# Reordering the last MLP pass of an encoder kernel: up and down visits, norm sums issued later, last squares summed by fp32 matmuls

## Chip, cores, metric

The kernel runs on the 8 cores of one Trainium2 chip. Every core computes two of the 16 sequences. The metric is device time in microseconds (us) of the slowest core. A program on all cores has a fast and a slow state: in the slow one the cores of a die are granted a lower clock (0.918 against 0.998 in the slow run of the result below). Fast runs are compared with fast runs here.

Most of the evidence is a shorter measure, read from each core's trace: **the last stretch**, from the first Relu of the last pass to the end of the core's span. Everything that the change touches lies in it, but for one memset of 0.17 us just before, and it repeats within 0.2 us over the eight cores of one execution of the kernel before or after, whereas the whole span varies by 4 to 6 us over cores, because the cores reach the last pass at different times.

## The reference, cut to what matters

```python
def rms_norm(x, g):
    y = xf * lax.rsqrt(jnp.mean(xf * xf, axis=-1, keepdims=True) + EPS)
    return (y * g).astype(x.dtype)

x = x + sq_relu_mlp(h, w_up, w_down)     # a = relu(h @ w_up);  (a * a) @ w_down
return rms_norm(x, norm_final)           # D_MODEL 1024, D_FF 4096, SEQ 2048
```

The kernel does the MLP in four passes of 1024 hidden channels. A pass visits four groups of 512 positions, each with an `up` and a `down` (8 tiles of 8 matmuls). In the last pass each `down` tile ends with the final residual add, and the final norm follows. The norm needs the sum of the squares over the 1024 channels, which lie in 8 chunks of 128 partitions, so the sum over partitions is a matmul with ones. The last group goes down in two halves of 256 positions.

## The kernel before

```python
def norm_sq(k, src, n=512, ns=0, eng='pool', lag=False, bufs=None):   # chunk k of 8
    # (cut: views of acc_, hi, lo, sq_)
    act(sq_[k % 2][:, 0:n] if k else acc_, src, AF.Square)            # ScalarE
    # (cut: the unused lag)
    add(k)                                                            # GpSimd: acc_ += sq_
    if k == 7:
        act(hi, acc_, AF.Copy)                                        # bf16 part
        tt('dve', lo, acc_, hi, ALU.subtract)                         # the rest, bf16

def norm_rstd(n=512, ns=0, r=None):                                   # "the sums"
    mm(o, ones, hi[:, 0:n], True, False)
    mm(o, ones, lo[:, 0:n], False, True)
    act(r, o, AF.Ln, scale=1.0 / D, bias=eps)
    act(r, r, AF.Exp, scale=-0.5)

def popp(fc, first=3, steps=2):      # after tile fc: `steps` pieces of pending work, from tile `first` on
    ...

def down(p_, tg, t0=0, n=512):
    first = 1 + last_seq if p_ == 3 else 3
    for fc in range(8):
        # (cut: 8 matmuls into o)
        tt('dve', x_, o, x_, ALU.add)                                 # VectorE: the add
        if p_ == 3:
            norm_sq(fc, x_, n, 0 if n == 512 else t0 // 256)
        popp(fc, first)

def fin_out(tg, t0=0, n=512, b_=b_):                                  # pending work of a finished group
    norm_rstd(n, ns, r)
    yield
    for c in range(8):
        stt(x_, x_, gains[:, 4, c:c + 1], r, ALU.mult, ALU.mult)      # VectorE: a scaling
        # (cut: every second chunk a store)
        yield

# last pass of the last sequence
for tg in range(NTG):
    up(3, tg)
    if tg:
        down(3, tg - 1)
        pend.append(fin_out(tg - 1))
for t0 in (0, 256):
    down(3, 3, t0, 256)
    pend.append(fin_out(3, t0, 256))
flush()
```

The softmax here doesn't subtract the row's maximum and nothing guards it: scores larger than these inputs give would overflow.

## Time and profile before

| | before |
|---|---|
| recorded runs | 2020.15, 2088.87, 1993.32 us, median 2020.15 |
| profiled run | 1995.15 us, fast; spans of the cores 1987.8 to 1994.1 us |
| last stretch | 132.8 us (132.7 to 132.9 over the cores) |
| of it: first Relu to last add | 121.2 us |
| of it: last add to the end | 11.6 us |

The page (slowest core, 5), busy time of TensorE, and shares of the chain of work that ended last:

```profile
PE 1957.0 (98%) x10234; PEld 968.8 (49%) x10234; DVE 963.5 (48%) x1585; ACT 773.3 (39%) x1291; POOL 417.5 (21%) x384
...
PE 93%; DVE 2%; SPq 1%; DMA 1%; issue 1%; ACT 1%; POOL 0%; DVEq 0%; ACTq 0%; POOLq 0%
```

TensorE (PE) bounds the kernel as a whole. The same chain from 1950 us on, by engine:

```profile
by line: DVE arena L149 29.9%; PE ps L149 19.9%; issue 15.9%; ACT arena L149 14.3%; POOL arena L149 7.7%; DVEq L143 1.5%; ACTq L143 0.5%; POOLq L143 0.3%
```

The timeline of TensorE (columns: start, length, engine, line, operation, tiles and shape, count, then in brackets the idle time before and what ended it):

```profile
1889.80 69.69 PE L149 MATMUL ps<-arena 128*128 128x512 bf16 x334
1960.89 0.38 PE L149 MATMUL ps<-arena 128*128 128x512 bf16 x1 [1.40 <-ACT arena L149]
1961.71 7.36 PE L149 MATMUL ps<-arena 128*128 128x512 bf16 x65 [0.45 <-DVE arena L149]
1974.26 0.37 PE L149 MATMUL ps<-arena 128*128 128x256 bf16 x1 [5.19 <-ACT arena L149]
1974.82 6.20 PE L149 MATMUL ps<-arena 128*128 128x256 bf16 x41 [0.18 <-DVE arena L149]
1985.09 0.86 PE L149 MATMUL ps<-arena 128*128 128x256 bf16 x2 [4.07 <-ACT arena L149]
```

Two waits stand out: at 1959.5 for hi and lo of group 2, at 1969.1 for those of the first half of group 3. After the second, 41 matmuls take 6.20 us where 65 had taken 7.36: their records start 0.213 us apart instead of 0.109 until 1978.1. The granted clock in three stretches (columns: stretch, length, busy time and count of TensorE, weight loads, VectorE, ScalarE, GpSimd, then granted clock, DMA share, GB/s):

```profile
1790.00:1887.00 97.00, 97.00 (x452) 43.94 (x450) 30.47 (x56) 18.51 (x31) 1.59 (x3) 1.00 0.18 33
1962.00:1969.00 7.00, 7.00 (x65) 6.09 (x63) 5.02 (x10) 3.12 (x7) 3.54 (x4) 1.00 0.19 77
...
1975.00:1982.00 7.00, 6.02 (x41) 4.61 (x39) 5.45 (x15) 3.11 (x8) 3.56 (x5) 0.78 0.22 75
```

The end on VectorE: adds (arena<-ps,arena, they read PSUM), scalings (SCALAR_TENSOR_TENSOR), and one lo (bf16<-f32).

```profile
1977.22 0.64 DVE L149 SCALAR_TENSOR_TENSOR arena<-arena 128x256 f32<-128x256 f32 x1 [1.55 <-ACT arena L149]
1977.79 0.41 DVE L149 TENSOR_TENSOR arena<-ps,arena 128x256 f32<-128x256 f32 x1
1978.12 0.87 DVE L149 SCALAR_TENSOR_TENSOR arena<-arena 128x256 f32<-128x256 f32 x2
1978.91 0.41 DVE L149 TENSOR_TENSOR arena<-ps,arena 128x256 f32<-128x256 f32 x1
...
1982.42 0.41 DVE L149 TENSOR_TENSOR arena<-ps,arena 128x256 f32<-128x256 f32 x1
1985.01 0.43 DVE L149 TENSOR_TENSOR arena<-arena 128x256 bf16<-128x256 f32 x1 [2.17 <-ACT arena L149]
1987.20 3.26 DVE L149 SCALAR_TENSOR_TENSOR arena<-arena 128x256 f32<-128x256 f32 x8 [1.77 <-ACT arena L149]
```

From 1977.22 to the last add at 1982.42 VectorE never idles: two scalings and an add per tile. The start of the last stretch, on ScalarE:

```profile
1861.25 0.60 ACT L149 ACTIVATE arena<-ps 128x512 bf16<-128x512 f32 x1 [28.76 <-PE ps L149]
```

So on this core the last stretch is 1994.1 - 1861.25 = 132.8 us, and the last add comes 1982.42 - 1861.25 = 121.2 us after its start.

### The profile page before, as it was taken

To read this page: it belongs to the slowest core of one execution; us is meant where nothing else is said; L and a number is where in the kernel's file an instruction comes from. 1 tells how busy PE (TensorE), PEld (TensorE's weight loads), DVE (VectorE), ACT (ScalarE), POOL (GpSimd) and SP (SyncE) were. 2 spreads that over 40 slices of the span, in tenths; PEclk is the share of its full clock that TensorE was granted. 3 is DMA by queue.
4 is the path that set the end of the run, shared out by engine and by line. 5 is a ranking of instruction groups with operands and counts; after the bars stand their busy time and mean duration, and the time that the engine had idled before them with its cause. 6 is when DMAs were issued, how large, how long until landed. Compare 5 with 4: busy or idle time off the path is not lost.

```text
span 1994.1 us, 30646 instructions; the slowest of 8 cores (1987.8 to 1994.1 us)
## 1 busy us (share of the span) xinstructions
PE 1957.0 (98%) x10234; PEld 968.8 (49%) x10234; DVE 963.5 (48%) x1585; ACT 773.3 (39%) x1291; POOL 417.5 (21%) x384
## 2 busy tenths in 40 slices
PE   8999999999999999999999999999999999999996
PEld 4456544554444444444445664446444444444443
DVE  5955643455553333336764456335556332323355
ACT  6355742455431332213325557235554112021243
POOL 3001042531310321101420002344133000000034
PEclk9999999999999999999999999999999999999998
DMA  9472352663012525043372440635600040222112
GB/s 239 85 138 64 54 139 73 106 110 60 1 64 43 118 69 110 22 79 116 102 198 60 86 81 23 189 59 96 121 1 1 1 79 6 46 40 43 22 75 95
DMA packets 51738, 155.41 MB, mean 78 GB/s; under 512 B 4993, under 2 KB 15362, under 8 KB 42114
## 3 DMA queue, kind: packets, MB, share of 16 engines
q0 software_dynamic: 14416, 75.50, 22.2%
q1 hardware_dynamic: 37026, 77.94, 12.6%
q8 instruction: 86, 1.41, 0.3%
q14 instruction: 66, 0.54, 0.1%
q10 hardware_dynamic: 144, 0.02, 0.0%
HBM read 205.87 MB, written 16.78 MB: 112 GB/s over the span
## 4 chain that ended last, share of the span: by engine, by line
PE 93%; DVE 2%; SPq 1%; DMA 1%; issue 1%; ACT 1%; POOL 0%; DVEq 0%; ACTq 0%; POOLq 0%
PE ps L149 93%; DVE arena L149 2%; SPq L149 1%; DMA arena<-x 1%; ACT arena L149 1%; DMA arena<-arena 0%; POOL arena L149 0%; SPq L147 0%; DVEq L143 0%; ACTq L143 0%; POOLq L143 0%; SPq L143 0%
## 5 line engine op out<-in xcount | busy, mean ns | idle before, releaser
L149 PE MATMUL ps<-arena 128*128 128x512 bf16 (+4 forms) x10234 | 1957.0, 354 | 28.9 <-ACT arena L149 12.0
L149 PEld LDWEIGHTS ps<-arena 128*128 128x128 bf16 (+1 forms) x10234 | 968.8, 100 | 1016.8 <-issue 70.1
L149 ACT ACTIVATE arena<-ps 128x512 bf16<-128x512 f32 (+3 forms) x776 | 472.4, 631 | 869.7 <-PE ps L149 747.7
L149 DVE TENSOR_TENSOR arena<-arena 128x512 bf16<-128x512 bf16 (+8 forms) x597 | 305.9, 532 | 479.3 <-ACT arena L149 466.5
L149 POOL TENSOR_TENSOR arena<-arena 128x512 f32<-128x512 f32 (+2 forms) x289 | 358.2, 1242 | 697.4 <-ACT arena L149 484.5
L149 DVE TENSOR_TENSOR arena<-ps,arena 128x512 f32<-128x512 f32 (+4 forms) x394 | 280.2, 722 | 280.2 <-PE ps L149 270.6
L149 ACT ACTIVATE arena<-arena 128x512 f32<-128x512 f32 (+6 forms) x460 | 282.4, 625 | 299.8 <-DVE arena L149 198.3
L149 DVE SCALAR_TENSOR_TENSOR arena<-arena 128x512 bf16<-128x512 f32 (+3 forms) x312 | 215.6, 730 | 37.8 <-ACT arena L149 37.3
L149 POOL DMA_DIRECT2D arena<-wb x62 | 33.8, 547 | 641.2 <-PE ps L149 602.7
L149 DVE SCALAR_TENSOR_TENSOR arena<-arena,ps 128x512 f32<-128x512 f32 x128 | 80.6, 683 | 126.9 <-PE ps L149 121.3
L149 DVE SCALAR_TENSOR_TENSOR arena<-ps,arena 128x512 f32<-128x512 f32 x64 | 43.5, 687 | 32.9 <-PE ps L149 32.9
L149 ACT ACTIVATE arena<-ps,arena 128x512 f32<-128x512 f32 (+3 forms) x50 | 29.2, 585 | 40.1 <-PE ps L149 35.6
L149 DVE COPY arena<-ps 128x1024 f32<-128x1024 f32 (+3 forms) x20 | 20.2, 1010 | 37.6 <-PE ps L149 37.6
L149 POOL DMA_DIRECT2D arena<-wa x23 | 15.6, 683 | 106.9 <-PE ps L149 87.2
L149 POOL MEMSET arena<- 128x2048 bf16 x6 | 10.8, 1808 | 120.8 <-PE ps L149 120.8
L149 DVE CAST arena<-ps 128x512 bf16<-128x512 f32 (+1 forms) x30 | 19.6, 667 | 12.1 <-PE ps L149 12.0
L149 DVE STREAM_SHUFFLE arena<-arena 128x2048 bf16<-128x2048 bf16 x6 | 13.7, 2287 | 0.0
L149 ACT ACT_TABLE_LOAD x5 | 6.4, 1283 | 4.1 <-DVE arena L149 4.1
L149 DVE TENSOR_SCALAR arena<-arena 128x512 bf16<-128x512 f32 x12 | 6.1, 516 | 3.3 <-DMA arena<-x 3.2
L149 DVE LOAD_MASK_SELECT arena<-arena x6 | 0.1, 14 | 13.2 <-DMA arena<-arena 13.1
L149 DVE MEMSET arena<- 128x1 bf16 (+3 forms) x7 | 0.9, 135 | 3.3 <-DMA arena<-gains 2.1
L149 DVE CAST arena<-arena 128x1 bf16<-128x1 f32 (+1 forms) x9 | 1.4, 160 | 0.4
(4 smaller groups left out, 0.4 us busy)
## 6 DMA issues: line engine op xcount, KB each, us to landing
arena<-wb POOLq DMA_DIRECT2D x62, 1024.0 KB, 9.9
arena<-x SPq DMA_DIRECT2D x8, 2048.0 KB, 24.5
arena<-x SPq DMA_DIRECT2D x32, 512.0 KB, 3.8
out<-arena SPq DMA_DIRECT2D x28, 512.0 KB, 2.8
arena<-wa POOLq DMA_DIRECT2D x17, 512.0 KB, 9.5
arena<-x SPq DMA_DIRECT2D x32, 256.0 KB, 14.7
arena<-rope SPq DMA_DIRECT2D x6, 1024.0 KB, 6.4
arena<-arena SPq DMA_DIRECT2D x96, 64.0 KB, 2.3
```

Of the source, the lines that this page charges most:

```text
L149: ins = getattr(eo, o['name'])(*o['args'], **o['kw'])
```

## The change

Four parts, all in the last pass of the last sequence. The visits become up0, up1, down0, up2, down1, down2, up3, down3, so that group 2's scalings run beside up3, and 14 of down3's matmuls are issued ahead of the last squared tile. The sums are issued later in TensorE's order (after tile 3 or 4 instead of 2). One chunk of the first half and three of the second go into the sums by fp32 matmuls with fp32 ones instead of GpSimd adds. One scaling per tile instead of two in the halves.

```diff
+        ones32_ = view(OFF['Y'] + 12 * KB, 128, F32)
+        sq_last = [[view(OFF['Y'] + (3 * i + k) * KB, 256, F32) for k in range(3)] for i in range(2)]
+            if k == (6 if direct == 3 else 8):
+                split()                                   # hi, lo
+            if k >= 8 - direct:
+                act(sq_last[ns][k - 8 + direct][:, 0:n], src, AF.Square)
+            elif k: ...                                   # Square, GpSimd add
+            if k == 7 and direct < 3:
+                split()
             mm(o, ones, hi[:, 0:n], True, False)
-            mm(o, ones, lo[:, 0:n], False, True)
+            mm(o, ones, lo[:, 0:n], False, direct == 0)
+            for k in range(direct):
+                mm(o, ones32_, sq_last[ns][k][:, 0:n], False, k == direct - 1)
...
-                first = 1 + last_seq if p_ == 3 else ...
+                first = (4 if tg == 3 else 2) if p_ == 3 and last_seq else ...      # in up
...
+                late = direct == 1
+                if late:
+                    for fc in range(2):
+                        tile_mm(fc, range(7))
-                    popp(fc, first)
+                    popp(fc, first, 1 if direct else 2)
...
-                yield
+                for _ in range(2 if direct else 1):
+                    yield
...
+                up(3, 0)
+                for tg in range(NTG - 1):
+                    if tg < NTG - 2:
+                        up(3, tg + 1)
+                    down(3, tg)
+                    pend.append(fin_out(tg))
+                up(3, 3)
+                for k, direct in enumerate((1, 3)):
+                    down(3, 3, 256 * k, 256, k, 3, direct)
+                    pend.append(fin_out(3, 256 * k, 256, k, direct))
```

(Cut: views, `tile_mm`, which issues the matmuls of one tile, the memset of the fp32 ones, and the old loop. Other passes and the first sequence keep their order.)

More of the change, by code (lines that the diff above doesn't have):

```diff
@@ L327, in wdma, with norm_sq, split, norm_rstd @@
             return dma('pool', dst, src, 'w%d' % (wn[0] % 10), after)
-        def norm_sq(k, src, n=512, ns=0, eng='pool', lag=False, bufs=None):
+        ones32_ = view(OFF['Y'] + 12 * KB, 128, F32)
+        sq_last = [[view(OFF['Y'] + (3 * i + k) * KB, 256, F32) for k in range(3)] for i in range(2)]
+        def norm_sq(k, src, n=512, ns=0, bufs=None, direct=0):
             acc_, (hi, lo) = nset[ns]
             acc_, hi, lo = acc_[:, 0:n], hi[:, 0:n], lo[:, 0:n]
-            sq_ = sq if bufs is None else bufs
-            def add(i):
-                if i > 0:
-                    tt(eng, acc_, acc_, sq_[i % 2][:, 0:n], ALU.add)
-            act(sq_[k % 2][:, 0:n] if k else acc_, src, AF.Square)
-            if lag and k:
-                add(k - 1)
-            if not lag or k == 7:
-                add(k)
-            if k == 7:
+            sq_ = (sq if bufs is None else bufs)[k % 2][:, 0:n]
+            def split():
                 act(hi, acc_, AF.Copy)
                 tt('dve', lo, acc_, hi, ALU.subtract)
-        def norm_rstd(n=512, ns=0, r=None):
+            if k == (6 if direct == 3 else 8):
+                split()
+            if k >= 8 - direct:
+                act(sq_last[ns][k - 8 + direct][:, 0:n], src, AF.Square)
+            elif k:
+                act(sq_, src, AF.Square)
+                tt('pool', acc_, acc_, sq_, ALU.add)
+            else:
+                act(acc_, src, AF.Square)
+            if k == 7 and direct < 3:
+                split()
+        def norm_rstd(n=512, ns=0, r=None, direct=0):
             r = (rstd if r is None else r)[:, 0:n]
@@ L1207, in up @@
             def up(p_, tg, hook=None):
-                first = 1 + last_seq if p_ == 3 else 6 if p_ + tg == 0 else 3
+                first = (4 if tg == 3 else 2) if p_ == 3 and last_seq else 1 if p_ == 3 else 6 if p_ + tg == 0 else 3
                 for fc in range(8):
@@ L1220, in up, with down, tile_mm, fin_out @@
                     popp(fc, first)
-            def down(p_, tg, t0=0, n=512):
-                first = 1 + last_seq if p_ == 3 else 3
+            def down(p_, tg, t0=0, n=512, ns=0, first=None, direct=0):
+                if first is None:
+                    first = 1 + last_seq if p_ == 3 else 3
                 tn = slice(t0, t0 + n)
-                for fc in range(8):
-                    w = bslot(17 + 4 * p_ + fc // 4).rearrange("p (k j) -> p k j", k=8)
-                    b = P.bank()
-                    o = psf(b)[:, 0:n]
-                    for dc in range(8):
-                        mm(o, w[:, dc, (fc % 4) * 128:(fc % 4 + 1) * 128], a2T[tg % 2][:, dc, tn], dc == 0, dc == 7)
+                bank = {}
+                late = direct == 1
+                def tile_mm(fc, dcs):
+                    if fc not in bank:
+                        bank[fc] = P.bank()
+                    w = bslot(17 + 4 * p_ + fc // 4).rearrange("p (k j) -> p k j", k=8)
+                    for dc in dcs:
+                        mm(psf(bank[fc])[:, 0:n], w[:, dc, (fc % 4) * 128:(fc % 4 + 1) * 128], a2T[tg % 2][:, dc, tn], dc == 0, dc == 7)
+                if late:
+                    for fc in range(2):
+                        tile_mm(fc, range(7))
+                for fc in range(8):
+                    tile_mm(fc, (7,) if late and fc < 2 else range(8))
                     x_ = xT[:, tg, fc, tn]
-                    tt('dve', x_, o, x_, ALU.add)
+                    tt('dve', x_, psf(bank[fc])[:, 0:n], x_, ALU.add)
                     if p_ == 3:
-                        norm_sq(fc, x_, n, 0 if n == 512 else t0 // 256)
-                    popp(fc, first)
+                        norm_sq(fc, x_, n, ns, direct=direct)
+                    popp(fc, first, 1 if direct else 2)
             rstd2 = view(Y0 + 8192, 512, F32)
-            def fin_out(tg, t0=0, n=512, b_=b_):
+            def fin_out(tg, t0=0, n=512, ns=0, direct=0, b_=b_):
                 tn = slice(t0, t0 + n)
-                ns = 0 if n == 512 else t0 // 256
                 r = (rstd, rstd2)[ns][:, 0:n]
-                norm_rstd(n, ns, r)
-                yield
+                norm_rstd(n, ns, r, direct)
+                for _ in range(2 if direct else 1):
+                    yield
                 for c in range(8):
@@ L1323, in build_program @@
                 aload(1)
+            if last_seq:
+                OP('dve', 'memset', ones32_, 1.0, writes=[ones32_])
+                up(3, 0)
[8 more added lines that the diff above has]
+                    pend.append(fin_out(3, 256 * k, 256, k, direct))
+                flush()
+                continue
             for tg in range(NTG):
                 up(3, tg)
-                if not last_seq:
-                    pend.append(fin_next(tg))
-                    if tg == 3:
-                        aload(2)
-                        aload(3)
+                pend.append(fin_next(tg))
+                if tg == 3:
+                    aload(2)
+                    aload(3)
                 if tg:
@@ L1333, in build_program @@
                     pend.append(fin_out(tg - 1))
-            if last_seq:
-                for t0 in (0, 256):
-                    down(3, 3, t0, 256)
-                    pend.append(fin_out(3, t0, 256))
-                flush()
-            else:
-                down(3, 3)
-                flush()
-                pend.append(fin_out(3))
-                load_rope(0)
-                for i in range(4, 8):
-                    aload(i)
+            down(3, 3)
+            flush()
+            pend.append(fin_out(3))
+            load_rope(0)
+            for i in range(4, 8):
+                aload(i)
         sems = []
```

## The prediction

> **What bounds it.** TensorE: busy 98% of the 1994.1 us span (page), 93% of the chain that ended last. Only the last 40 us are loose. In the last pass of the last sequence TensorE is dense until 1959.5. The waits view from 1880 on gives it 7.2 us idle in two places: 1.4+0.45 us at 1959.5 (sums of position group 2, issued three 256-wide tiles after that group's last add) and 5.2 us at 1969.1 (sums of group 3's first half, same distance). Behind the second gap matmuls start 0.213 us apart instead of 0.109 until 1978.1: the half clock after idleness of the Trainium skill, "TensorE: Matmul & The Clock Gate", Part 1; the trace agrees (PEclk 0.78 there). That costs another 1.7 us. VectorE, given two scalings per tile, is then 1.4 us behind: last matmul ends 1981.0, last add starts 1982.4. Then (timeline): square, two GpSimd adds (0.73 us each), hi, lo, two matmuls, Ln, Exp; scalings start 1987.2, 4.8 us after that add, take 3.3 us; the store lands 3.6 us later.
>
> **What changes.**
> 1. Group 3's up comes after group 2's down, so group 2's sums are issued five up tiles (8.6 us) after their chain starts, which needs about 4: that gap goes. Group 3's down now follows its up at once; the last squared tile is ready about 1.3 us after the last up matmul, and 14 matmuls held before it cover 1.5: 0 to 0.3 us lost.
> 2. The first half's sums come after four tiles (3.5 us) and the chain is shorter: chunk 7's square by one fp32 matmul instead of a GpSimd add, hi/lo ready about 2 us after the last matmul. The 5.2 us and the half clock go.
> 3. One scaling per tile, from tile 5: no VectorE backlog.
> 4. Second half: chunks 5 to 7 by fp32 matmuls; hi/lo done during the visit. After the last add: square 0.42, one fp32 matmul, Ln 0.47, Exp 0.42.
>
> **Costs added.** Four fp32 matmuls of 256 columns. The kernel's start has 512-column ones: two records 0.50 us apart, 1.09 together, against 0.216 bf16 spacing; the skill's "FP8 and Floating Point Precision" gives four passes, which agrees. Estimate 0.5 us each. One lies on the dense path, two run beside add and square, one in the tail. Five left-over scalings of the first half (2 us on VectorE) fall in the tail beside square, matmul, Ln, Exp: 0 to 0.3 us.
>
> **Sum (slowest core).** Down of group 3 starts 1957.1, 128 matmuls at 0.109, plus 0.75 for the first half's sums: last matmul ends 1972.1 (8.9 earlier); last add 1972.2 (10.2 earlier); scalings about 2.9 after it instead of 4.8: 1975.1; then 3.3 + 3.6 unchanged: 1982. About 12 us, 0.6%, all on the critical path.
>
> **Predicted**: 1982.5 us in the fast state (before, fast: 1993 to 1995), 1979 to 1987 there. The recorded 2020 median of before contains slow runs; if after's does too, it reads about 12 us under its like. So the range is 1979 to 2010. Faster by over 2%: 0.03; within 2%: 0.96; slower: 0.01.
>
> **What would show it.** TensorE waits after 1950 down from 7.2 us to under 1, apart from the tail; clock 0.99 in the 15 us before the last add, at 1972 to 1973; GpSimd absent from the final chain, one fp32 matmul in its place; last add to first scaling about 3 us.
>
> **What would make it wrong.** The 14 held matmuls don't cover; fp32 matmuls slower than estimated; VectorE behind in group 2's down (0.69 + two scalings 1.41 exceeds 1.73 us per tile); left-over scalings or their stores delaying the final ones; GpSimd behind in the first half, so that its sums wait.

## The result

| | before | after |
|---|---|---|
| median of all runs | 2007.09 us (4) | 1984.09 us (4) |
| those at the fast level | 1993.32, 1994.03 | 1983.35, 1984.77, 1983.4, and 1985.58, which the median leaves out |
| ratio of fast runs, 95% interval | | 0.9953 (0.9929 to 0.9977) |
| the same, later with more rounds | | 0.9956 (0.9943 to 0.9970) |
| last stretch, every core | 132.8 us | 123.5 us |
| first Relu to last add | 121.2 us | 113.6 us |
| last add to the end | 11.6 us | 9.9 us |

A ratio is the mean time of one kernel's fast runs over that of the other's, the 1985.58 us counted too, so not quite the ratio of the medians. The gain is 9.3 us in the last stretch, on each of the eight cores, and 9.3 of 1993.7 us is the 0.47% of the ratio. One of the new kernel's runs was slow (2139.22 us: die 0 at a clock of 0.918, die 1 at 0.998); it is left out.

After (slowest core, 4), the start of the last stretch on ScalarE:

```profile
1858.76 0.60 ACT L149 ACTIVATE arena<-ps 128x512 bf16<-128x512 f32 x1 [28.76 <-PE ps L149]
```

The timeline of TensorE after:

```profile
1939.76 9.68 PE L149 MATMUL ps<-arena 128*128 128x512 bf16 x43
1949.89 7.08 PE L149 MATMUL ps<-arena 128*128 128x512 bf16 x39 [0.45 <-DVE arena L149]
1957.27 13.37 PE L149 MATMUL ps<-arena 128*128 128x256 bf16 x118 [0.29 <-DVE arena L149]
1971.72 0.27 PE L149 MATMUL ps<-arena 128*128 128x256 bf16 x1 [1.08 <-ACT arena L149]
1972.21 1.91 PE L149 MATMUL ps<-arena 128*128 128x256 bf16 x7 [0.22 <-DVE arena L149]
```

The waits of 1.4 and 5.2 us are gone, and no matmul before the tail runs at the half clock. What is left: a small wait for group 2's lo at 1949.4, one at 1957.0 where the held matmuls have run out, and 1.08 us for hi at 1970.6, after the last visit. The first of them is a little longer than its bracket: matmul records overlap, and single records show a start 0.83 us after the one before where 0.216 is usual, so 0.6 us is lost; in the second 0.46 us (0.567 instead of 0.109).

GpSimd in the last two visits (six and four adds):

```profile
1959.77 5.35 POOL L149 TENSOR_TENSOR arena<-arena 128x256 f32<-128x256 f32 x6 [11.68 <-ACT arena L149]
1967.61 3.35 POOL L149 TENSOR_TENSOR arena<-arena 128x256 f32<-128x256 f32 x4 [2.49 <-ACT arena L149]
```

Within each half it adds without a pause, about 0.9 us from start to start, as long as TensorE takes for a tile (8 matmuls of 0.109 us); between the halves it waits 2.49 us. VectorE, in group 2's down, between the halves and at the end:

```profile
1938.17 0.68 DVE L149 TENSOR_TENSOR arena<-ps,arena 128x512 f32<-128x512 f32 x1
1938.77 2.87 DVE L149 SCALAR_TENSOR_TENSOR arena<-arena 128x512 f32<-128x512 f32 x2
1941.56 0.68 DVE L149 TENSOR_TENSOR arena<-ps,arena 128x512 f32<-128x512 f32 x1
...
1965.86 0.43 DVE L149 TENSOR_TENSOR arena<-arena 128x256 bf16<-128x256 f32 x1 [2.45 <-ACT arena L149]
1966.21 1.41 DVE L149 TENSOR_TENSOR arena<-ps,arena 128x256 f32<-128x256 f32 x4
...
1970.29 0.42 DVE L149 TENSOR_TENSOR arena<-ps,arena 128x256 f32<-128x256 f32 x1
1971.63 0.43 DVE L149 TENSOR_TENSOR arena<-arena 128x256 bf16<-128x256 f32 x1 [0.93 <-ACT arena L149]
1971.98 0.48 DVE L149 SCALAR_TENSOR_TENSOR arena<-arena 128x256 f32<-128x256 f32 x1
1972.37 0.42 DVE L149 TENSOR_TENSOR arena<-ps,arena 128x256 f32<-128x256 f32 x1
1972.71 2.45 DVE L149 SCALAR_TENSOR_TENSOR arena<-arena 128x256 f32<-128x256 f32 x6
1975.37 3.25 DVE L149 SCALAR_TENSOR_TENSOR arena<-arena 128x256 f32<-128x256 f32 x8 [0.20 <-ACT arena L149]
```

The line at 1965.86 is the first half's lo. VectorE idles 2.45 us before it, and the second half's first adds stand behind it, although that half's first tile had its last matmul at 1963.49: this is why GpSimd, which needs their squares, pauses between the halves. The line at 1971.63 is the second half's lo. It stands before the last add (1972.37) in VectorE's order, and it waits for hi, which waits for GpSimd. The last matmul of the visit had started at 1970.36, so its add could have begun at about 1970.7. And two scalings at 1938.77 take 2.87 us where two usually take 1.41. The chain from 1950 on:

```profile
by line: DVE arena L149 17.6%; POOL arena L149 17.0%; ACT arena L149 11.9%; issue 11.2%; PE ps L149 4.9%; DVEq L143 1.0%; POOLq L143 0.4%; ACTq L143 0.3%
```

GpSimd's (POOL) share rose from 7.7% to 17.0%: it was predicted to leave the chain, and now stands level with VectorE's 17.6% at the front of it.

### The profile page after: what moved, and what is told of

The parts are those of the page before. It is cut to its first block, busy times and chain, and to the rows that moved or that the text cites. A ratio compares the mean times of both kernels' runs of the same rounds, so it can differ in the third digit from the quotient of the medians.

```text
span 1982.3 us, 30478 instructions; the slowest of 8 cores (1978.4 to 1982.3 us)
## 1 busy us (share of the span) xinstructions
PE 1944.4 (98%) x10062; PEld 968.3 (49%) x10242; DVE 963.9 (49%) x1586; ACT 772.5 (39%) x1291; POOL 414.1 (21%) x380
## 3 DMA queue, kind: packets, MB, share of 16 engines
q8 instruction: 86, 1.41, 0.3%
## 4 chain that ended last, share of the span: by engine, by line
PE 92%; DVE 3%; issue 2%; DMA 1%; ACT 1%; POOL 1%; SPq 0%; DVEq 0%; ACTq 0%; POOLq 0%
PE ps L149 92%; DVE arena L149 3%; ACT arena L149 1%; DMA arena<-x 1%; POOL arena L149 1%; DMA arena<-arena 0%; SPq L149 0%; DVEq L143 0%; SPq L147 0%; ACTq L143 0%; POOLq L143 0%; SPq L143 0%
## 5 line engine op out<-in xcount | busy, mean ns | idle before, releaser
L149 PE MATMUL ps<-arena 128*128 128x512 bf16 (+3 forms) x10062 | 1944.4, 353 | 29.7 <-DVE arena L149 11.4
L149 DVE SCALAR_TENSOR_TENSOR arena<-arena,ps 128x512 f32<-128x512 f32 x128 | 80.5, 683 | 126.9 <-PE ps L149 121.3
## 6 DMA issues: line engine op xcount, KB each, us to landing
arena<-wb POOLq DMA_DIRECT2D x62, 1024.0 KB, 10.2
```

The costliest lines, as they stand in the source:

```text
L149: ins = getattr(eo, o['name'])(*o['args'], **o['kw'])
```

## The experiments

**Theory.** Before, VectorE's scalings bound the last two visits, not TensorE's half clock. After, what keeps the last add from being as early as predicted is the second half's lo in VectorE's queue (waiting for GpSimd), and GpSimd's adds stretching the scalings in group 2's down. **Rivals**: TensorE (fp32 matmuls, clock), or VectorE's scalings by their number, still bound it. What bound the kernel before is tested from one side only: warm_before rules the half clock out, but no run thins the scalings in the old order, and its VectorE also idles for the sums' chain (2.24 us before the first half's lo at 1974.25, 1.55 us before the scaling at 1977.22). All fourteen runs gave correct results. "Stretch" is the last stretch, "last add" the time from its first Relu; both are means over the cores.

### Which part of the change brings what

**order_only**: the new order, but sums at the old depth, no fp32 matmuls, two scalings per tile (cut: a line that keeps the held matmuls).

```diff
-                first = (4 if tg == 3 else 2) if p_ == 3 and last_seq else ...
+                first = 2 if p_ == 3 and last_seq else ...
-                for k, direct in enumerate((1, 3)):
-                    down(3, 3, 256 * k, 256, k, 3, direct)
+                for k in range(2):
+                    down(3, 3, 256 * k, 256, k, 2, 0)
```

> Measured by the last stretch: from the first Relu of the last pass to the end of the core's span, 132.8 us before and 123.5 us after on every core. Here only the visit order is new (with the matmuls held before the last squared tile); sums stay two tiles deep, no fp32 matmuls, two scalings per tile. Theory (order and depth are both needed): group 2's sums wait about 3 us, the first half's about 2 us, last stretch 128 to 131 us. Rival (the order alone brings the gain): at most 125 us.

Measured: stretch 131.7 us (131.0 to 132.7), 0.7 us past the expected range; last add 120.0. The order alone brings 1.1 us. Waits of TensorE from 1860 on (who waited for whom, us in total, times, longest):

```profile
PE ps L149 <- ACT arena L149: 9.2, 3, 5.6
PE ps L149 <- DVE arena L149: 0.5, 2, 0.3
```

The longest, 5.6 us, is the tail. Of the other two, one of 3.3 us is for group 2's hi; the first half's, expected at 2 us, is only 0.3. In the last visit VectorE carries two scalings and an add per tile and starts its last add 3.0 us after TensorE's last matmul of the visit has ended. The rival falls.

**old_order**: all but the order (the first half keeps two scalings per tile, as group 2's eight have to fit in it; cut here: that, and that no matmuls are held).

```diff
-                    if tg < NTG - 2:
-                        up(3, tg + 1)
+                    up(3, tg + 1)
                     down(3, tg)
                     pend.append(fin_out(tg))
-                up(3, 3)
```

> Old visit order; sums one tile deeper, fp32 matmuls (1 and 3 chunks), one scaling per tile in the second half. Theory: group 2's eight 512-wide scalings (0.75 us each) then still stand beside the first half's adds on VectorE, which falls behind by 3 us or more: last stretch 126 to 129 us. Rival (depth and fp32 bring the gain, the order nothing): at most 124.5 us.

Measured: stretch 129.1 us (128.8 to 129.5), last add 119.2, tail 9.9; just past the expected range. Without the order the rest brings 3.7 us, 1.7 of them in the tail. The parts alone bring 1.1 + 3.7 = 4.8 of 9.3 us: they need each other.

**no_fp32**: order, depth and pace, no fp32 matmuls.

```diff
-                for k, direct in enumerate((1, 3)):
-                    down(3, 3, 256 * k, 256, k, 3, direct)
+                for k in range(2):
+                    down(3, 3, 256 * k, 256, k, 3, 0)      # paced as in the new kernel
```

> The new kernel with its order, depth and pace, but all eight squares summed by GpSimd in both halves. Theory (GpSimd's adds, 0.87 us apart, are the chain that bounds the last two visits): TensorE waits over 1 us for the first half's sums, and the last stretch is 125.5 to 127 us. Rival (GpSimd has slack during the visits, only the tail gets longer, by two adds and hi/lo less one fp32 matmul): 124.5 to 125.2 us with the last add at 113.6 as in the new kernel.

Measured: stretch 125.9 us, inside the theory's range, but its reason was half wrong: TensorE waits only 0.4 us for the first half's sums, and the last add comes at 113.25, earlier than the new kernel's 113.6, which fits that lo no longer stands before it. The tail is 2.8 us longer (12.7 against 9.9). So the fp32 matmuls work in the tail; up to the last add they bring nothing.

**shallow**: the new kernel, sums at the old depth.

```diff
-                first = (4 if tg == 3 else 2) if p_ == 3 and last_seq else ...
+                first = 2 if p_ == 3 and last_seq else ...
-                    down(3, 3, 256 * k, 256, k, 3, direct)
+                    down(3, 3, 256 * k, 256, k, 2, direct)
```

> The new kernel with its sums back at the old depth (two tiles, also for group 2). Theory (with the new order, group 2's chain is late because VectorE is behind in its down, so depth is what the order needs): TensorE waits about 3.3 us for group 2's sums, last stretch 125.5 to 127. Rival (fp32 has shortened the chains enough for the old depth): at most 124.3.

Measured: stretch 127.5 us (126.9 to 128.3), half a microsecond more than expected; TensorE waits 3.3 us once, for group 2's hi. Depth is worth 4.0 us with this order.

**two_scalings**: the new kernel with two scalings per tile in the halves.

```diff
-                    popp(fc, first, 1 if direct else 2)
+                    popp(fc, first, 2)
```

> The new kernel with two scalings of the older half per tile instead of one. Theory (the last add is held by lo, and the tail by sums and left-over scalings alike, so the pace matters little): last stretch 123.3 to 124.3. Rival (one scaling per tile is what keeps VectorE in time): 124.8 or more.

Measured: stretch 125.25 us (124.8 to 125.5), last add 115.0. My theory missed and the rival holds: the pace is worth 1.7 us. The wait for the second half's hi on TensorE is 2.00 us instead of 1.08:

```profile
1973.87 0.27 PE L149 MATMUL ps<-arena 128*128 128x256 bf16 x1 [2.00 <-ACT arena L149]
```

### Was the half clock a cost?

**warm_before**: the kernel before, with matmuls without use in the 5.2 us gap.

```diff
+                if n == 256 and t0 == 0:
+                    for _ in range(46):
+                        mm(psf(wb_)[:, 0:256], ones, hT[:, 0, 0:256], True, True)
                 norm_rstd(n, ns, r)
```

> The kernel before, with 46 matmuls without use in the 5.2 us gap, so that the clock does not fall. Theory (VectorE with its scalings and adds, not TensorE, bounds the last half visit before): the 0.213 us spacings are gone and the last stretch stays 132.8 us within 0.3. Rival (my prediction: the half clock costs 1.7 us): about 131.1 us.

Measured: stretch 132.9 us, last add 121.2, both as before. TensorE around the filled gap:

```profile
1972.88 0.27 PE L149 MATMUL ps<-arena 128*128 128x256 bf16 x1 [0.18 <-issue]
1973.43 4.64 PE L149 MATMUL ps<-arena 128*128 128x256 bf16 x41 [0.29 <-DVE arena L149]
1983.70 0.86 PE L149 MATMUL ps<-arena 128*128 128x256 bf16 x2 [5.63 <-ACT arena L149]
```

The 41 matmuls take 4.64 us instead of 6.20, and TensorE then waits 5.63 us instead of 4.07: the same sum. The half clock comes with the idle gap, as the Trainium skill, "TensorE: Matmul & The Clock Gate", Part 1, has it, and goes when the gap is filled, but it cost nothing here. The traces of before had said so already: its cores show 11 to 38 matmuls at the half clock, and all have the last add at 121.2 to 121.3.

### What holds the last add after the change

**late_scalings**: no scaling of the first half before the last add.

```diff
-                for _ in range(2 if direct else 1):
+                for _ in range(5 if direct else 1):
```

> No scaling of the first half before the last add; all eight follow it. Theory (lo holds the last add): last add at most 0.5 us earlier than 113.6, stretch 123.5 to 124.4. Rival (VectorE's scalings hold it): last add at least 1 us earlier.

Measured: last add 113.2 (0.4 earlier), stretch 123.6. As the theory says; the scalings do not hold the last add.

**fp32_3_3** and **fp32_1_5**: fewer GpSimd adds in the first or in the second half.

```diff
-                for k, direct in enumerate((1, 3)):
+                for k, direct in enumerate((3, 3)):      # fp32_1_5: (1, 5), hi/lo at chunk 4
```

> Three fp32 chunks in both halves: GpSimd has two adds less in the first half, TensorE two fp32 matmuls more (1.1 us). Theory (GpSimd's chain of the first half holds up the squares of the second, whose lo subtract then holds the last add on VectorE by 1.6 us): last add about 0.5 us earlier than the new kernel's 113.6, last stretch about 123.0. Rival (TensorE is the limit up to the last add): last add and stretch 1.1 us later, 124.6.

> Five fp32 chunks in the second half instead of three: GpSimd has two adds there instead of four. Theory (the second half's lo, late because of GpSimd, holds the last add): last add 1.4 to 1.6 us earlier (about 112.1), last stretch 122.6 to 123.0. Rival (VectorE's scalings hold the last add): last add unchanged, and the stretch 124.5 by the two matmuls more.

Measured: (3, 3): last add 113.45, stretch 123.3, a gain of 0.15 where 0.5 was expected; the two matmuls more are paid for, and hardly more. (1, 5): stretch 122.8 as expected, last add 112.9, half of the expected step. VectorE in (1, 5):

```profile
1969.68 0.43 DVE L149 TENSOR_TENSOR arena<-arena 128x256 bf16<-128x256 f32 x1 [1.34 <-ACT arena L149]
1970.02 0.42 DVE L149 TENSOR_TENSOR arena<-ps,arena 128x256 f32<-128x256 f32 x1
...
1971.47 0.42 DVE L149 TENSOR_TENSOR arena<-ps,arena 128x256 f32<-128x256 f32 x1
```

lo now stands before three adds instead of one and still waits, so the adds and scalings behind it queue up. That explains the half step; it is read from these lines only.

**lo_last**: the same new kernel, lo after the last add.

```diff
             def split():
                 act(hi, acc_, AF.Copy)
-                tt('dve', lo, acc_, hi, ALU.subtract)
+                if direct < 3:
+                    tt('dve', lo, acc_, hi, ALU.subtract)
...
+            if k == 7 and direct == 3:
+                tt('dve', lo, acc_, hi, ALU.subtract)
```

> The new kernel with the second half's lo subtract placed after the last add on VectorE, nothing else moved. Theory (lo's place in VectorE's queue holds the last add, waiting for GpSimd's sum): last add 112.1 to 112.4 after the first Relu instead of 113.6; the sums still wait for lo, so the last stretch gains only 0.2 to 0.5 us: 123.0 to 123.3. Rival (GpSimd's load, not lo's place, holds the adds): last add 113.2 or more.

Measured: last add 112.4, stretch 123.15, both in the theory's ranges. Moving one instruction brings the last add 1.2 us forward; the sums still wait for lo, so the end gains only 0.35.

```profile
1971.02 0.41 DVE L149 TENSOR_TENSOR arena<-ps,arena 128x256 f32<-128x256 f32 x1
1971.49 0.42 DVE L149 TENSOR_TENSOR arena<-arena 128x256 bf16<-128x256 f32 x1
1971.83 2.46 DVE L149 SCALAR_TENSOR_TENSOR arena<-arena 128x256 f32<-128x256 f32 x6
```

**bf16_group2**: GpSimd out of group 2's down alone.

```diff
+            if direct == 8:
+                act(sq8[k], src, AF.Square)               # bf16
+                return
...
+            for k in range(8 if direct == 8 else 0):
+                mm(o, ones, sq8[k], k == 0, k == 7)
```

> The new kernel with group 2's squares in bf16, summed by eight 512-wide bf16 matmuls: no GpSimd add beside group 1's scalings. Theory (GpSimd's adds block the scalings, which made VectorE 2.2 us later in group 2's down and gave TensorE the 0.6 us wait for group 2's lo): all eight scalings of group 1 take about 0.75 us instead of up to 1.8, the wait is gone, and TensorE has 1.3 us of matmuls more: last stretch 124.0 to 124.4. Rival (VectorE is late by the number of its instructions alone): the scalings stay stretched or the wait stays at 0.4 us or more, last stretch 124.6 or more.

Measured: stretch 124.0 us and last add 114.1, both 0.5 us later than in the new kernel, as the 1.3 us of added matmuls cost more than the wait did; TensorE's wait for group 2's sums is gone; the scalings in group 2's down are all 0.75 us long or 1.41 for two, and VectorE's last add there comes 2.4 us earlier:

```profile
1937.70 0.69 DVE L149 TENSOR_TENSOR arena<-ps,arena 128x512 f32<-128x512 f32 x1
1938.30 1.41 DVE L149 SCALAR_TENSOR_TENSOR arena<-arena 128x512 f32<-128x512 f32 x2
1939.62 0.69 DVE L149 TENSOR_TENSOR arena<-ps,arena 128x512 f32<-128x512 f32 x1
```

So GpSimd's adds did stretch them. In the new kernel a scaling that starts at 1939.85 ends at 1941.64, 0.55 us after the GpSimd add that runs from 1939.83 to 1941.09: it looks blocked, not slowed. All cores say the same: 40 scalings of the new kernel's end (five per core) start while a GpSimd add runs, last 1.02 to 1.80 us, and each ends 0.55 us after that add. The Trainium skill, "SBUF — State Buffer", section "SBUF: two separate sides", says that a VectorE instruction with two SBUF inputs and a GpSimd instruction that reads SBUF share a port pair by an exclusive lock. The trace agrees: adds that read PSUM, with one SBUF input, stay at 0.68 us beside the same GpSimd adds. One thing this run doesn't part: it also takes away the lo for which TensorE waited. That the stretching alone made the 0.6 us wait is worked out (VectorE is 2.4 us earlier without it), not shown.

### A version without GpSimd and lo in the last visits

**bf16_squares**: all eight squares of both halves in bf16, summed by eight bf16 matmuls.

```diff
+            if direct:
+                act(sq_b[ns][k], src, AF.Square)          # bf16
+                return
...
+            if direct:
+                for k in range(8):
+                    mm(o, ones, sq_b[ns][k], k == 0, k == 7)
```

> In both last halves ScalarE writes all eight squares in bf16 and TensorE sums them with eight bf16 matmuls of 0.109 us; no GpSimd add, no hi/lo, no fp32 matmul. Theory (GpSimd and lo hold the last add by 1.6 us): last add about 112.0, last stretch about 121.5, the whole 0.55 to 0.6% under the kernel before. Rival (TensorE or the scalings hold the last add): last add 113.6, stretch 123 or more. The result should stay right within the tolerance, the rounding of single squares averaging out over 1024.

Measured: last add 112.1, stretch 121.7, ratio to before 0.9945 (0.9929 to 0.9962), result correct. The last add is 1.5 us earlier than in the new kernel: that is what GpSimd and lo cost there, net of the eight bf16 matmuls (0.87 us a half) that replace hi, lo and fp32 ones (0.65 us in the first half).

**new_again** and **bf16_paced**, on one chip in five rounds: the new kernel again, and bf16_squares with group 2's sums one tile later and three tiles held instead of two.

```diff
-                first = (4 if tg == 3 else 2) if ...
+                first = (5 if tg == 3 else 2) if ...
-                    for fc in range(2):
+                    for fc in range(3):
                         tile_mm(fc, range(7))
```

> The new kernel unchanged, with more rounds. The last stretch (first Relu of the last pass to the end) was 9.3 us shorter than before on every core; if the last stretch is all that differs, the ratio of fast runs is 0.9953, between 0.9940 and 0.9962. Rival (the 11.8 us between the slowest cores of the first two profiles): 0.9941 or less.

> The bf16 squares of both last halves, and group 2's sums one tile later, and three tiles instead of two held before the last squared tile. Theory (the 0.6 us wait for group 2's lo and the 0.46 us at the start of group 3's down are what TensorE still loses): both waits gone, last add about 111.1 after the first Relu, last stretch 120.6 to 121.0, ratio of fast runs to before about 0.994. Rival (VectorE, still busy with group 2's scalings, holds the first adds and the chain behind them): last stretch 121.3 or more.

Measured: new_again 0.9956 (0.9943 to 0.9970), stretch 123.5; two of its six runs were slow (2100.79 and 2376.75 us). The theory's 0.9953 lies in the interval, the rival's 0.9941 does not. bf16_paced: last add 111.0, stretch 120.6 on every core, 0.9936 (0.9923 to 0.9950), median 1981.06 us. From 1939.7, in group 2's down, TensorE is dense to the last matmul but one (some records are missing from the count):

```profile
1939.70 31.31 PE L149 MATMUL ps<-arena 128*128 128x512 bf16 x215
1971.44 0.27 PE L149 MATMUL ps<-arena 128*128 128x256 bf16 x1 [0.42 <-ACT arena L149]
```

The scalings in group 2's down are still stretched here, to the same 1.8 us: issuing the sums later hides the stretch without removing it. This version is 2.9 us shorter in the last stretch than the new kernel and 12.2 us shorter than the one before. By whole times its interval overlaps with new_again's, so the stretch decides between those two. It drops the care for precision of hi/lo and fp32 in the last group only.

## Why the prediction was right or wrong

Right, by the runs: the two waits and their end; the place of the gain (the last 40 us); the tail (predicted 1.9 us shorter, measured 1.75; last add to first scaling "about 3 us", measured 3.00); the time in the fast state, 1984 us, within 1979 to 1987.

Wrong:

1. **The term "last add 1972.2 (10.2 earlier)"** is the mis-sized one. It is 111.0 us after the first Relu (1972.2 - 1861.2); measured 113.6, so 7.6 us earlier, not 10.2. "About 12 us" became 9.3. The sum took TensorE as dense and put nothing in for the engines that feed it. The missing 2.6 us are found: 113.6 - 112.1 = 1.5 for GpSimd and lo before the last add (bf16_squares; lo_last shows 1.2 for lo's place alone), and 112.1 - 111.0 = 1.1 for the two waits at group 2's sums and at the held matmuls (bf16_paced, which removes both at once). With both taken away the last add is at 111.0, the predicted place.
2. **"hi/lo done during the visit"** and **"GpSimd absent from the final chain"** failed. GpSimd had ten adds, about 0.9 us from start to start, as slow as a tile. It began late, because VectorE, at group 2's scalings, started the first add at 1958.36, 0.8 us after the first tile's last matmul had ended (1957.27 + 0.27), and it never caught up in that half. So the first half's lo came late, and it held the second half's first adds until 1966.21, 2.4 us after the first tile's matmuls had ended (1963.49 + 0.27); GpSimd began the second half late too, and that half's lo then blocked the last add. The second step is shown by lo_last; the first is read from the trace, as no run moves the first half's lo alone. The prediction had "GpSimd behind in the first half" among its dangers, and costed it at nothing.
3. **"That costs another 1.7 us"** (half clock) failed: warm_before removes it and gains nothing. VectorE was the limit there, and the wait only moved.
4. **"14 matmuls ... cover"** and the 8.6 us for group 2's sums against "about 4": both nearly, but not quite. 0.46 and 0.6 us were lost. The first, by the trace, because two of group 2's scalings (1955.38 to 1956.78) stood before the last squared tile on VectorE, whose Relu had ended at 1956.19. The second at least in part because group 1's scalings ran beside GpSimd's adds in group 2's down; the prediction named VectorE's load there (0.69 + 1.41 us), not the blocking (up to 1.79 us for one scaling, gone in bf16_group2).
5. **The figure on the last line was a fast-state time, held against a mixed one.** 1982.5 against the recorded 2020.15 reads as 1.9% faster, against the fast 1993 to 1995 as 0.6%; measured between fast runs 0.47%. The text knew this and widened the range, but one number cannot say both. A forecast should be stated as a ratio of fast runs first.

One of its tests passed by luck: "last add at 1972 to 1973" came true at 1972.37, but on another core, whose last pass had begun 2.5 us earlier. So did the span of the slowest core, 1982.3 us where the sum gave 1982. Absolute times of different runs should be set against a common mark before they are compared. The estimate of 0.5 us for an fp32 matmul of 256 columns was a little high: two records 0.216 us apart, 0.43 us.

## What to carry to other kernels

At the end of a kernel, where the bound engine runs out of other work, count every helper engine per tile: a helper that needs as long per tile as the matmuls (here GpSimd, about 0.9 us) cannot make up a late start during the visit. Look at what stands behind a waiting instruction in its engine's order; a small subtract for a later sum can hold the add that everything waits for. An idle or slowed engine is a cost only if removing it moves the next event, which a run with filler work shows cheaply.

## What the Trainium skill lacked or had wrong

- "SBUF — State Buffer" (SBUF: two separate sides) states the lock between GpSimd and VectorE; no page gives its size for these two instructions: a 512-wide fp32 scaling took 0.75 us alone and up to 1.80 us beside GpSimd adds of 1.27 us, and ended 0.55 us after the add that blocked it.
- "FP8 and Floating Point Precision" (TensorE Precision Notes) gives four passes for true fp32, not the time: here 0.43 us for 256 columns, four times the bf16 spacing of 0.109 us, in two records.
- "TensorE: Matmul & The Clock Gate" (Back-to-back issue gap) gives about 131 ns as the sustained spacing at 512 columns; here the 97 dense us from 1790 to 1887 before the change hold 452 matmuls of that width, 0.215 us each, which is the figure that this section gives for an isolated one.
- The same page (Part 1) says that dense matmuls on three or more cores of a die take that die to 13/16 (0.81) of the clock and hold it there; here all eight cores, with TensorE 98% busy, were granted 0.993 to 0.999 over the whole kernel in every fast run. Only slow runs come near the page's figure: 0.811 to 0.845 on one die in the slowest (2333.15, 2376.75 and 2386.64 us), 0.918 in another.
